# Weight sums made in DRAM by accumulating DMA, for a Strassen form that only adds, and a projection half that begins with the kept weights

## The chip, the cores and the metric

The kernel runs on one core of one Trainium2 chip. The metric is device microseconds of one execution; a profile is one further execution, taken by the hardware profiler. The engines that matter here: TensorE (PE) multiplies, with its weight loads counted apart (PEld); VectorE (DVE), ScalarE (ACT) and GpSimd (POOL) work elementwise; SyncE (SP) computes nothing and issues most transfers. POOL issues some transfers on a queue of its own. Sixteen DMA engines carry all of them.

## The reference

One layer of a hybrid encoder is computed for two groups that share weights: a prompt of 1024 rows and a sample of 64 rows, 1088 columns in all in the kernel's transposed layout, model width 1024, float32.

- Conditioning: `mod = silu(c) @ w_ada + b_ada` gives shift, scale and gate for both sub-layers (adaLN).
- Token mixing: `u = rmsnorm(x) * (1 + sc1) + sh1`, `proj = u @ w_in`; from `proj` come a stick-breaking attention (8 heads of 64) and an mLSTM (4 heads of 128, in chunks). Both are projected (`w_a`, `w_b`), gated by sigmoids, merged, and `x = x + g1 * (merged @ w_out)`.
- Channel mixing: `u2 = rmsnorm(x) * (1 + sc2) + sh2`; `x = x + g2 * ((silu(u2 @ w_ff_gate) * (u2 @ w_ff_up)) @ w_ff_down)`, inner width 2816, which is 22 blocks of 128.
- A last rmsnorm. Keys, values, states and convolution rows are outputs too.

## The kernel before

Every product is made from pairs of fp32r tiles: a high part (a rounded copy, the helpers `hi_act`, L46, and `hi_pool`, L52) and a low part (the rest, `lo_dve`, L55, and `lo_pool`, L58), with three matmuls high-high, high-low, low-high (`mm3`, L74). A weight block of 1024 x 128 is loaded as a raw tile (tag `wr`, three buffers of 512 KB), then split into tags `wh` and `wl` (three buffers each).

**The order of the work** is not the program's order line by line. A planner walks the written program with costs of its own: each engine takes, whenever it is free in the plan, the instruction that comes first in the program among those whose inputs and buffers are ready. The result is a fixed order per engine; on the chip each engine keeps it and waits where it must.

**Start** (to about 72 us). The rows of x are loaded, normalised and transposed. The adaLN weights of the first two of six parts are loaded in blocks (`ada_blocks`, L180, tiles `wada`, ten buffers, L187), two blocks for each of the eight row blocks of the input (`ada_pair`). `make_u` (L271) modulates block kb and splits it into `uh` (POOL, L52) and `ul` (DVE, L55). The q and k units of mLSTM head 0 accumulate over kb as the blocks come. The gates' weights are loaded at L855.

**mLSTM stage** (to about 480 us). Four heads; for each, a consumer (`mlstm(h)`) is woven by `run` (L814) into a list of dense units: the attention's q, k, v of pair h (`qkv_units`, L792) and the mLSTM units of head h + 1 (`ml_units`, L797). A unit is one weight block against all columns in three chunks (`unit`, L313, load at L63). Then come the attention stage and the two branch projections.

**Output projection** (about 957 to 1079 us). The eight output blocks m are made twice: first for columns 0 to 543 (`wo_weights`, `residual`, `wo_half(m, 0, ...)`), then for the rest (`wo_half(m, 1, ...)`, loop at L1185), each half in two quarters of 272 columns (`wo_quarter`, L1043), with the residual add on DVE (L1051) and squares summed on POOL (L1059). In the second loop each weight block is loaded and split again (L1187). While it runs, `todo` modulates the first half for the FFN (`rstd_rows`, `modulate2`, L1130), one step after each quarter, and writes the seven operand pairs of a Strassen product (`split`, `ops`).

**Gate and up** (about 1079 to 1584 us). For each of the 22 FFN blocks i, the gate weights (A11, A12: the two row halves) and the up weights (A21, A22) form one 2 x 2 block matrix against the input's 2 x 2 blocks, and Strassen's form with seven products (Winograd's variant) is used: `order = (1, 6, 5, 7, 2, 3, 4)`. `load_pair` (L1207) loads the two raw tiles; `weight_op` (L1217) makes the sums S1, S2, S3 of weight quarters on POOL (L1228, L1229, L1235, L1240) and splits each of the seven weights with ACT and DVE; `gate_up` (L1253) issues 84 matmuls for one half of the columns (L1289) and recombines the products on DVE, ACT and POOL (L1264 to L1282), storing h to DRAM (L1283). The order of the 44 half jobs: blocks 0 to 9 first half, blocks 10 to 21 both halves, blocks 0 to 9 second half; so the weights of blocks 0 to 9 are made twice. The weights of the next job are made, one by one, after each product of the present job (`hook`). The modulation of the second column half is stepped in the first ten jobs at products 1, 5 and 2.

**Down projection and output** (to the end) are untouched by the change.

Of the kernel before, what the change touches and what calls it, by code (L numbers as in the profile page):

```python
# [8 lines left out]
F32 = mybir.dt.float32  # L9
# [5 lines left out]
P = 128  # L15
# [4 lines left out]
KB = 8  # L20
# [2 lines left out]
TILES = [(0, 64)] + [(64 + 128 * i, 128) for i in range(8)]  # L23
CTILES = [(0, 1, 2), (3, 4, 5), (6, 7, 8)]
FFB = 22
HT = T // 2
QT = T // 4
XW = 3 + NS + 3 + NP
# [6 lines left out]
def trunk(ctx, tc, a, o, dbg=None, stop=None):  # L35
# [9 lines left out]
    def hi_act(out, in_):  # L45
        nc.scalar.copy(out, in_)  # L46
# [23 lines left out]
    def cols(w, c0, n=P):  # L70

        return w[:, c0 : c0 + n].rearrange("(kb p) n -> p kb n", p=P)
# [72 lines left out]
    gb_d = dram.tile([KB, P, T], F32, name="gb_d")  # L145
    pb_d = dram.tile([KB, P, T], F32, name="pb_d")
    nm_d = dram.tile([36, P], F32, name="nm_d")

    def small(shape, name, tag, dtype=F32, bufs=2, pool=None):
        return (pool or cur["sb"]).tile(shape, dtype, tag=tag, name=name, bufs=bufs)  # L150
# [892 lines left out]
    def wo_quarter(m, q, ws):  # L1043
# [9 lines left out]
        if m == 0:  # L1053
# [4 lines left out]
        if m < KB - 1:  # L1058
            nc.gpsimd.tensor_add(acc[:, s:e], acc[:, s:e], sq)  # L1059
        return sq  # L1060

    def wo_half(m, h, ws, after):
        sq = []
        for i in range(2):
            sq.append(wo_quarter(m, 2 * h + i, ws))
            if i == 1:
                nc.sync.dma_start(x1_d[m][:, HT * h : HT * (h + 1)], x1v(m, HT * h, HT * (h + 1)))
            after()
        return sq

    def rstd(accs, c, name):
# [48 lines left out]

    ops = {}

    def split(h, jp, p, src):
# [4 lines left out]
    def modulate2(h, jp, r):  # L1130


        x = [x1t[h, jp, i] for i in range(2)]
        rr = r.rearrange("p i t -> p (i t)")
        for i in range(2):
            nc.vector.tensor_mul(x[i], x[i], rr[:, None, :].to_broadcast([P, 2, HT]))
# [11 lines left out]
        nc.vector.tensor_sub(t2, b22, b11)  # L1148
        split(h, jp, 5, b11)
        yield  # L1150
        nc.vector.tensor_sub(b11, b21, t2)
# [20 lines left out]
        next(gen, None)  # L1172

    order = (1, 6, 5, 7, 2, 3, 4)
    sqs = None
    for m in range(KB):
        ws, xr = wo_weights(m)
        for c in range(3):
            residual(m, c, xr)
        sqs = wo_half(m, 0, ws, lambda: None)  # L1180
# [4 lines left out]
    for m in range(KB):  # L1185
        raw = wp.tile([P, KB, P], F32, tag="wr", name=f"wr_wp{m}")
        nc.sync.dma_start(raw, cols(w_out, m * P))  # L1187
        ws = [wp.tile([P, KB, P], F32R, tag=t, name=f"{t}_wp{m}") for t in ("wh", "wl")]
        hi_act(ws[0], raw)
        lo_pool(ws[1], raw, ws[0])  # L1190
        sqs = wo_half(m, 1, ws, lambda: step(todo))
    for _ in todo:
        pass
    for p in order:
# [10 lines left out]
        return gp.tile([P, QT], F32, tag=tag, name=name, bufs=1)  # L1205

    def load_pair(i):  # L1207
        raws = []
        for w, nm in ((w_g, "g"), (w_u, "u")):
            raw = wp.tile([P, KB, P], F32, tag="wr", name=f"wr_{nm}{i}")  # L1210
            nc.sync.dma_start(raw, cols(w, i * P))
            raws.append(raw)
        return [raws[0][:, 0:4], raws[0][:, 4:8], raws[1][:, 0:4], raws[1][:, 4:8]]

    S = {}

    def weight_op(i, p, raw):  # L1217

        a11, a12, a21, a22 = raw

        def new(tag):
            return gp.tile([P, 4, P], F32, tag=tag, name=f"{tag}_{i}", bufs=1)

        if p == 1:
            src = a11
        elif p == 6:
            S[1], S[2] = new("S1"), new("S2")
            nc.gpsimd.tensor_add(S[1], a21, a22)  # L1228
            nc.gpsimd.tensor_sub(S[2], S[1], a11)  # L1229
            src = S[2]  # L1230
        elif p == 5:
            src = S[1]
        elif p == 7:
            src = new("S3")
            nc.gpsimd.tensor_sub(src, a11, a21)  # L1235
        elif p == 2:
            src = a12
        elif p == 3:
            src = new("S3")
            nc.gpsimd.tensor_sub(src, a12, S[2])  # L1240
        else:
            src = a22
        k = order.index(p)
        if k < 6:
            w = wp.tile([P, KB, P], F32R, tag="wh" if k < 3 else "wl", name=f"w{p}_{i}")
        else:
            w = npl.tile([P, T], F32R, tag="acc", name=f"w{p}_{i}", bufs=1)[:, : KB * P].rearrange("p (k n) -> p k n", n=P)
        w = w.rearrange("p (x j) n -> p x j n", x=2)
        hi_act(w[:, 0], src)
        lo_dve(w[:, 1], src, w[:, 0])  # L1250
        return w

    def gate_up(i, h, ws, after):  # L1253
# [7 lines left out]
        def evac(p):  # L1261
            if p == 1:
                t["p1"] = tq("p1", f"p1_{i}_{h}")
                nc.scalar.copy(t["p1"], ba)  # L1264
            elif p == 6:
                t["u2"] = tq("u2", f"u2_{i}_{h}")
                nc.vector.tensor_add(t["u2"], bb, t["p1"])
            elif p == 5:
                nc.vector.tensor_add(h1, bc, t["u2"])  # L1269
            elif p == 7:  # L1270
                nc.vector.tensor_add(h1, bd, h1)
            elif p == 2:
                t["g0"] = tq("g0", f"g0_{i}_{h}")
                nc.scalar.activation(t["g0"], ba, AF.Silu)
            elif p == 3:
                t["g1"] = tq("g1", f"g1_{i}_{h}")
                nc.vector.tensor_add(t["g1"], bc, t["u2"])
                nc.scalar.activation(t["g1"], t["g1"], AF.Silu)  # L1278
                nc.gpsimd.tensor_mul(h1, t["g1"], h1)  # L1279
            else:  # L1280
                nc.vector.tensor_add(h0, bd, t["u2"])  # L1281
                nc.vector.tensor_mul(h0, t["g0"], h0)  # L1282
                nc.sync.dma_start(h_d[i][:, HT * h : HT * (h + 1)], hst)  # L1283

        for p in order:
# [19 lines left out]
            yield  # L1305


    NF = 10
# [205 lines left out]
```

## Time and profile before

| | |
|---|---|
| three runs, median | 1879.35 us (1872.82 to 1879.62) |
| profiled execution | 1873.3 us, span 1871.6 us |
| mean granted TensorE clock | 0.978 |
| PE busy | 1774.8 us, 95% |
| DVE, ACT, POOL busy | 1010.6, 667.9, 812.6 us |
| read from DRAM, written to it | 171.46 MB, 56.83 MB |

A busy PE is not a PE at its peak: its matmuls overlap, and at a lowered clock each lasts longer. The number of matmuls in a stretch, set against the stretch's length, tells more. DMA share and GB/s of a stretch tell how full the DMA engines are. Waits are put down to the semaphore that came last.

### The profile page before, as it was taken

Reading aid. Unit: us, or ns where it says so; the run is one execution under the profiler, and the core shown is the slowest. Engines: PE = TensorE matmul, PEld = TensorE weight load, DVE = VectorE, ACT = ScalarE, POOL = GpSimd, SP = SyncE. Lnnn points to the kernel's source line nnn. Section 1 sums busy time; section 2 is a strip of 40 time slices with the busy share of each in tenths; the row PEclk is TensorE's granted clock in tenths of the full one; section 3 lists DMA queues with packets and bytes.
Section 4 is the critical chain, followed back from the end, with each engine's and each line's share of the span. In section 5 each row is a group of like instructions: output and inputs, shape, how many; then the busy total and the mean of one; then the engine's idle time right before and its main releaser. Section 6 shows DMA issues by size and latency. Waiting matters only on the chain. (4 is left out here: it accounts for less than half of the span.)

```text
span 1871.6 us, 31615 instructions
## 1 busy us (share of the span) xinstructions
PE 1774.8 (95%) x12388; PEld 1700.0 (91%) x12388; DVE 1010.6 (54%) x1859; ACT 667.9 (36%) x1404; POOL 812.6 (43%) x665
## 2 busy tenths in 40 slices
PE   6999999999899999979989988999999998999997
PEld 4799999999898888868989988999999988999997
DVE  6623324242367586876461888654444765444535
ACT  4423434342244444534223554432333443100006
POOL 3433435352423222496665645542233456354323
PEclk9999999999999999989999979999999999999999
DMA  9323433324855565764665323332223433543102
GB/s 274 100 87 92 111 92 103 101 84 138 180 139 133 146 145 143 200 203 137 197 193 158 93 75 103 115 98 70 76 70 93 139 110 112 191 144 115 58 12 96
DMA packets 277575, 230.36 MB, mean 123 GB/s; under 512 B 11830, under 2 KB 255794, under 8 KB 277426
## 3 DMA queue, kind: packets, MB, share of 16 engines
q1 hardware_dynamic: 271794, 210.51, 38.2%
q0 software_dynamic: 5632, 17.83, 4.3%
q8 instruction: 98, 1.61, 0.4%
q14 instruction: 51, 0.42, 0.1%
HBM read 171.46 MB, written 56.83 MB: 122 GB/s over the span
## 5 line engine op out<-in xcount | busy, mean ns | idle before, releaser
L77 PE MATMUL ps_fd<-hh,wl_fd 128*128 128x384 f32 (+1 forms) x480 | 157.3, 328 | 2.1 <-POOL wl_fd L58 2.1
L75 PE MATMUL ps_fd<-hh,wh_fd 128*128 128x384 f32 (+1 forms) x480 | 157.1, 327 | 0.6 <-DVE hst L1281 0.6
L76 PE MATMUL ps_fd<-hl,wh_fd 128*128 128x384 f32 (+1 forms) x480 | 157.0, 327 | 0.0
L55 DVE TENSOR_TENSOR w<-S,w 128x512 fp32r<-128x512 f32 x128 | 104.8, 833 | 61.5 <-ACT w L46 59.9
L46 ACT CAST w<-S 128x512 fp32r<-128x512 f32 x128 | 76.8, 619 | 134.4 <-POOL S L1229 44.3
L1366 DVE SCALAR_TENSOR_TENSOR x1f<-ps_fd,mod,x1f 128x384 f32<-128x384 f32 (+2 forms) x128 | 60.5, 497 | 101.7 <-PE ps_fd L77 101.6
L363 DVE TENSOR_TENSOR_SCAN re<-re 128x128 f32<-128x128 f32 (+3 forms) x64 | 106.7, 1670 | 15.9 <-ACT re L359 15.5
L1240 POOL TENSOR_TENSOR S<-wr_g,S 128x512 f32<-128x512 f32 x32 | 49.1, 1536 | 126.4 <-DVE w L55 126.4
L77 PEld LDWEIGHTS ps_fd<-hh,wl_fd 128*128 128x128 f32 x480 | 90.1, 188 | 2.4 <-POOL wl_fd L58 2.4
L75 PEld LDWEIGHTS ps_fd<-hh,wh_fd 128*128 128x128 f32 x480 | 90.1, 188 | 0.8 <-issue 0.8
L76 PEld LDWEIGHTS ps_fd<-hl,wh_fd 128*128 128x128 f32 x480 | 90.1, 188 | 0.0
L46 ACT CAST hh<-hr 128x1088 fp32r<-128x1088 f32 (+1 forms) x26 | 24.0, 961 | 177.5 <-PE ps_fd L76 148.0
L1289 PE MATMUL ps_gb<-b6h,w 128*128 128x272 f32 x352 | 78.4, 301 | 6.0 <-DVE w L55 3.2
L1289 PE MATMUL ps_gc<-b3h,w 128*128 128x272 f32 x352 | 76.3, 296 | 8.2 <-DVE hst L1269 7.7
L1289 PE MATMUL ps_ga<-b1h,w 128*128 128x272 f32 x352 | 75.1, 292 | 5.0 <-DVE x L1051 5.0
L1228 POOL TENSOR_TENSOR S<-wr_u 128x512 f32<-128x512 f32 x32 | 42.4, 1325 | 83.8 <-DMA wr_u<-in_w_ff_up 74.8
L359 ACT ACTIVATE re<-z 128x512 f32<-128x512 f32 (+2 forms) x96 | 47.3, 494 | 82.2 <-DVE z L355 66.5
L1289 PE MATMUL ps_gc<-b5h,w 128*128 128x272 f32 x352 | 76.2, 295 | 0.0
L1289 PE MATMUL ps_gd<-b7h,w 128*128 128x272 f32 x352 | 74.8, 291 | 0.8 <-ACT w L46 0.8
L1289 PE MATMUL ps_ga<-b2h,w 128*128 128x272 f32 x352 | 74.7, 290 | 0.0
L1289 PE MATMUL ps_gd<-b4h,w 128*128 128x272 f32 x352 | 73.7, 289 | 0.0
L1279 POOL TENSOR_TENSOR hst<-g,hst 128x272 f32<-128x272 f32 x44 | 37.1, 843 | 81.7 <-ACT g L1278 81.7
(544 smaller groups left out, 6223.1 us busy)
## 6 DMA issues: line engine op xcount, KB each, us to landing
wada<-in_w_ada SPq DMA_DIRECT2D x48, 512.0 KB
wr_g<-in_w_ff_gate SPq DMA_DIRECT2D x32, 512.0 KB
wr_u<-in_w_ff_up SPq DMA_DIRECT2D x32, 512.0 KB
h_d<-hst SPq DMA_DIRECT2D x44, 272.0 KB
wr_fd<-in_w_ff_down SPq DMA_DIRECT2D x20, 512.0 KB
hr<-h_d SPq DMA_DIRECT2D x18, 544.0 KB
qs<-qk_d POOLq DMA_DIRECT2D x16, 272.0 KB, 6.9
kh<-qk_d POOLq DMA_DIRECT2D x16, 272.0 KB, 4.3
```

What stands on the lines that cost most here:

```text
L46: nc.scalar.copy(out, in_)
L55: nc.vector.tensor_sub(out, in_, h.bitcast(F32))
L75: nc.tensor.matmul(ps, wh, xh, start=first, stop=False)
L76: nc.tensor.matmul(ps, wh, xl, start=False, stop=False)
L77: nc.tensor.matmul(ps, wl, xh, start=False, stop=last)
L359: nc.scalar.activation(rest[:, c0 : c0 + w], ps, AF.Sigmoid, scale=-scale)
L363: nc.vector.tensor_tensor_scan(r, r, r, 1.0, ALU.mult, ALU.bypass)
L1228: nc.gpsimd.tensor_add(S[1], a21, a22)
L1240: nc.gpsimd.tensor_sub(src, a12, S[2])
L1279: nc.gpsimd.tensor_mul(h1, t["g1"], h1)
L1289: nc.tensor.matmul(ps, w[:, a, j, :], b[j // 2][:, j % 2, :], start=p in (1, 6, 5, 7) and j == 0 and k == 0, stop=j == 3 and k == 2, skip_ ...
L1366: nc.vector.scalar_tensor_tensor(x1[m][:, lo:hi], ps[:, lo - s : hi - s], mod[:, 40 + m, g : g + 1], x1[m][:, lo:hi], ALU.mult, ALU.add)
```

## The change

Three parts.

1. For blocks 0 to 9 (the first 1280 columns of the gate and up weights) four sums of weight quarters are made once, in DRAM: `wsum1 = u1 + u2`, `wsum2 = g1 + wsum1`, `wsum3 = u1 + g1`, `wsum4 = g2 + wsum2`, where 1 and 2 are the upper and lower 512 rows. Each is a copy from DRAM to DRAM issued on SP (`sum_copy`, two transfers of 512 x 640) and an accumulating transfer issued on POOL (`sum_add`, two transfers). In the program they stand between the dense units of the mLSTM heads: all copies with head 0, the adds 1 and 3 with head 1, add 2 with head 2, add 4 with head 3. `load_pair` for these blocks loads seven quarters of 256 KB, three of them straight from the weights and four from the sums, into three `wr` tiles and the tile S1; `weight_op` then only splits.
2. The signs are changed so that the weight sums are sums alone: the block operands b and the recombination on DVE take the sign. The product that ends h for the second row half moves from POOL to DVE, and both closing products become scalar_tensor_tensor with -1. Blocks 10 to 21 still make their sums on POOL, as additions. The second half's modulation is stepped at products 6 and 2 of the first ten jobs.
3. The second loop of the output projection runs over m in the order 7, 6, 5, 0, 1, 2, 3, 4; for 7, 6 and 5 it uses the weight tiles that the first loop still holds. Three steps of `todo` are taken for each m in place of two.

```diff
+    wsum_d = {x: dram.tile([KH, NFC], F32, name=f"wsum{x}_d") for x in (1, 2, 3, 4)}
+    g1w, g2w, u1w, u2w = w_g[0:KH, 0:NFC], w_g[KH:D, 0:NFC], w_u[0:KH, 0:NFC], w_u[KH:D, 0:NFC]
+    sum_parts = {1: (u1w, u2w), 2: (g1w, wsum_d[1]), 3: (u1w, g1w), 4: (g2w, wsum_d[2])}
+    def sum_copy(x):
+        def go():
+            for c in range(0, NFC, NFC // 2):
+                nc.sync.dma_start(wsum_d[x][:, c : c + NFC // 2], sum_parts[x][0][:, c : c + NFC // 2])
...
+    def sum_add(x):
+        def go():
+            for c in range(0, NFC, NFC // 2):
+                nc.gpsimd.dma_start(wsum_d[x][:, c : c + NFC // 2], sum_parts[x][1][:, c : c + NFC // 2], accum_op=ALU.add)
...
     for h in range(4):
-        dense = qkv_units(h) + (ml_units(h + 1) if h < 3 else ada_left[0:2] + gates[0:2])
+        q_, k_, kp, v_, vp = qkv_units(h)
+        m_ = ml_units(h + 1) if h < 3 else ada_left[0:2] + gates[0:2]
+        b_ = [[sum_copy(1), sum_copy(3), sum_copy(2), sum_copy(4)], [sum_add(1), sum_add(3)], [sum_add(2)], [sum_add(4)]][h]
+        dense = []
+        for i, g in enumerate([q_, k_, kp, v_, vp] + m_):
+            dense += [g] + (b_[i // 2 : i // 2 + 1] if i % 2 == 0 else [])
         run(mlstm(h), chain(dense), 14, 23 if h < 3 else 17)
...
-        nc.vector.tensor_sub(b11, b12, b11)
+        nc.vector.tensor_sub(b11, b11, b12)
...
+    def some(i):
+        step(todo)
+        if i == 1:
+            step(todo)
+
+    again = (7, 6, 5, 0, 1, 2, 3, 4)
+    for m in again:
+        ws = kept[m]
+        if m < 5:
+            raw = wp.tile([P, KB, P], F32, tag="wr", name=f"wr_wp{m}")
+            nc.sync.dma_start(raw, cols(w_out, m * P))
...
+        sqs = wo_half(m, 1, ws, m == again[0], m == again[-1], some)
...
+        src = {1: half(w_g, 0), 6: half(wsum_d[2], 0), 5: half(wsum_d[1], 0), 7: half(wsum_d[3], 0),
+               2: half(w_g, 1), 3: half(wsum_d[4], 0), 4: half(w_u, 1)}
+        for k in range(4):
+            if k < 3:
+                raw = wp.tile([P, KB, P], F32, tag="wr", name=f"wr_{k}_{i}")
+            else:
+                raw = gp.tile([P, 4, P], F32, tag="S1", name=f"wr_{k}_{i}", bufs=1)
+            for x, p in enumerate(order[2 * k : 2 * k + 2]):
+                res[p] = raw[:, 4 * x : 4 * x + 4]
+                nc.sync.dma_start(res[p], src[p])
...
-        if p == 1:
-            src = a11
+        if i < NF or p in (1, 2, 4):
+            src = raw[p]
...
-                nc.gpsimd.tensor_mul(h1, t["g1"], h1)
+                nc.vector.scalar_tensor_tensor(h1, h1, -1.0, t["g1"], ALU.mult, ALU.mult)
             else:
                 nc.vector.tensor_add(h0, bd, t["u2"])
-                nc.vector.tensor_mul(h0, t["g0"], h0)
+                nc.vector.scalar_tensor_tensor(h0, h0, -1.0, t["g0"], ALU.mult, ALU.mult)
...
-            if (k < NF and p in (1, 5, 2)) or (k >= FFB and p == 5):
+            if (k < NF and p in (6, 2)) or (k >= FFB and p == 5):
                 step(todo)
```

More of the change, by code (lines that the diff above doesn't have):

```diff
@@ L1041, in residual, with wo_quarter @@
             nc.scalar.copy(x1v(m, lo, hi), pst[:, lo - s : hi - s])
-    def wo_quarter(m, q, ws):
+    def wo_quarter(m, q, ws, first, last):
         (wh, wl), s, e = ws, QT * q, QT * (q + 1)
@@ L1052, in wo_quarter @@
         x = x1v(m, s, e)
-        if m == 0:
+        if first:
             nc.scalar.activation(acc[:, s:e], x, AF.Square)
@@ L1057, in wo_quarter, with wo_half @@
         nc.scalar.activation(sq, x, AF.Square)
-        if m < KB - 1:
+        if not last:
             nc.gpsimd.tensor_add(acc[:, s:e], acc[:, s:e], sq)
         return sq
-    def wo_half(m, h, ws, after):
+    def wo_half(m, h, ws, first, last, after):
         sq = []
         for i in range(2):
-            sq.append(wo_quarter(m, 2 * h + i, ws))
+            sq.append(wo_quarter(m, 2 * h + i, ws, first, last))
             if i == 1:
                 nc.sync.dma_start(x1_d[m][:, HT * h : HT * (h + 1)], x1v(m, HT * h, HT * (h + 1)))
-            after()
+            after(i)
         return sq
@@ L1184, in trunk @@
     todo = chain([rstd_rows(0, sqs, rows2[0], sbank), modulate2(0, 0, rows2[0]), modulate2(0, 1, rows2[0])])
[L1185 to L1191, printed above, removed]
+    def some(i):
[8 more added lines that the diff above has]
+            nc.sync.dma_start(raw, cols(w_out, m * P))
+            ws = [wp.tile([P, KB, P], F32R, tag=t, name=f"{t}_wp{m}") for t in ("wh", "wl")]
+            hi_act(ws[0], raw)
+            lo_pool(ws[1], raw, ws[0])
+        sqs = wo_half(m, 1, ws, m == again[0], m == again[-1], some)
     for _ in todo:
@@ L1207, in load_pair, with half @@
     def load_pair(i):
[L1208 to L1213, printed above, removed]
+        def half(w, r):
+            return w[r * KH : (r + 1) * KH, i * P : (i + 1) * P].rearrange("(k p) n -> p k n", p=P)
+        res = {}
+        if i >= NF:
+            raws = []
+            for w, nm in ((w_g, "g"), (w_u, "u")):
+                raw = wp.tile([P, KB, P], F32, tag="wr", name=f"wr_{nm}{i}")
+                nc.sync.dma_start(raw, cols(w, i * P))
+                raws.append(raw)
+            res[1], res[2], res[0], res[4] = raws[0][:, 0:4], raws[0][:, 4:8], raws[1][:, 0:4], raws[1][:, 4:8]
+            return res
+        src = {1: half(w_g, 0), 6: half(wsum_d[2], 0), 5: half(wsum_d[1], 0), 7: half(wsum_d[3], 0),
[8 more added lines that the diff above has]
+                nc.sync.dma_start(res[p], src[p])
+        return res
     S = {}
     def weight_op(i, p, raw):
[L1219 removed]
         def new(tag):
             return gp.tile([P, 4, P], F32, tag=tag, name=f"{tag}_{i}", bufs=1)
[L1224 to L1225 removed]
+        if i < NF or p in (1, 2, 4):
+            src = raw[p]
         elif p == 6:
             S[1], S[2] = new("S1"), new("S2")
[L1228 to L1229 removed]
+            nc.gpsimd.tensor_add(S[1], raw[0], raw[4])
+            nc.gpsimd.tensor_add(S[2], S[1], raw[1])
             src = S[2]
@@ L1234, in weight_op @@
             src = new("S3")
[L1235 to L1238, printed above, removed]
+            nc.gpsimd.tensor_add(src, raw[1], raw[0])
+        else:
             src = new("S3")
-            nc.gpsimd.tensor_sub(src, a12, S[2])
-        else:
-            src = a22
+            nc.gpsimd.tensor_add(src, raw[2], S[2])
         k = order.index(p)
```

22 lines of the change are left out of this document (15 added, 7 removed).

## The prediction

> **What bounds the kernel now.** I read the page first, for the share of each engine, and then the windows, stage by stage, because a kernel whose TensorE (PE) is 95% busy can only change where PE is not fed.
>
> ```profile
> span 1871.6 us, 31615 instructions
> PE 1774.8 (95%) x12388; PEld 1700.0 (91%) x12388; DVE 1010.6 (54%) x1859; ACT 667.9 (36%) x1404; POOL 812.6 (43%) x665
> ```
>
> In the windows a row begins with the stretch and its length; then come busy time and instruction count for PE, its weight loads, DVE, ACT and POOL; then the granted clock, the DMA share and GB/s. These rows go from the end of the second projection half through the whole gate/up stage:
>
> ```profile
> 1033.00:1074.00 41.00, 41.00 (x329) 40.85 (x328) 38.27 (x38) 25.23 (x48) 25.90 (x17) 1.00 0.33 100
> 1074.00:1079.50 5.50, 0.48 (x5) 0.29 (x3) 4.85 (x7) 1.88 (x5) 5.04 (x5) 0.77 0.14 51
> 1079.50:1101.00 21.50, 21.50 (x135) 21.14 (x136) 13.63 (x24) 11.87 (x22) 5.47 (x5) 0.74 0.21 62
> 1101.00:1143.00 42.00, 33.36 (x233) 32.04 (x232) 41.97 (x56) 24.55 (x46) 19.93 (x14) 0.90 0.26 77
> 1143.00:1206.00 63.00, 61.98 (x467) 61.18 (x466) 45.87 (x76) 26.30 (x54) 34.59 (x27) 0.96 0.40 119
> 1206.00:1227.00 21.00, 20.11 (x152) 19.12 (x152) 11.12 (x22) 6.95 (x16) 11.48 (x10) 1.00 0.45 128
> 1227.00:1480.00 253.00, 253.00 (x2015) 253.00 (x2014) 128.54 (x239) 85.01 (x169) 81.42 (x72) 1.00 0.28 86
> 1480.00:1584.00 104.00, 98.93 (x741) 94.05 (x740) 66.43 (x115) 41.03 (x85) 54.55 (x44) 1.00 0.40 116
> ```
>
> The undisturbed row is 1227 to 1480: 2015 matmuls in 253 us, 125.6 ns each, so a half job of 84 takes 10.55 us. I price every other row by its count, since "busy" hides slow matmuls. The loss is 5.5 - 5 x 0.1256 = 4.9 us, then 4.5, 12.7, 4.3, 1.9, and 10.9 in the last row: 39.2 us. The projection (1033 to 1074) loses nothing. Two causes show. From 1101 to 1143 DVE is busy 41.97 of 42 us: it is the bound. And its instructions are stretched there, as the groups of the same two windows show (mean ns after the comma), first the crowded stretch, then the calm one:
>
> ```profile
> L55 DVE TENSOR_TENSOR w<-S,w 128x512 fp32r<-128x512 f32 x10 | 9.6, 971 | 0.0
> ...
> L55 DVE TENSOR_TENSOR w<-S,w 128x512 fp32r<-128x512 f32 x51 | 36.7, 720 | 9.3 <-ACT w L46 8.7
> ```
>
> In the last ten half jobs the bound is a chain instead: the load of the up weights lands late, and three POOL sums of 1.29 us follow before ACT and DVE can split them.
>
> ```profile
> L1240 POOL TENSOR_TENSOR S<-wr_g,S 128x512 f32<-128x512 f32 x8 | 14.0, 1747 | 13.7 <-DVE w L55 13.7
> L1229 POOL TENSOR_TENSOR S<-S,wr_g 128x512 f32<-128x512 f32 x8 | 10.3, 1292 | 0.0
> L1235 POOL TENSOR_TENSOR S<-wr_g,wr_u 128x512 f32<-128x512 f32 x8 | 10.3, 1289 | 0.0
> L1228 POOL TENSOR_TENSOR S<-wr_u 128x512 f32<-128x512 f32 x8 | 10.3, 1288 | 22.8 <-DMA wr_u<-in_w_ff_up 16.9 <-DVE hst L1271 5.9
> ```
>
> The start is a third kind of stretch. The first row is mostly the rows of x, the second the adaLN weights, the third what comes behind them:
>
> ```profile
> 4.00:14.00 10.00, 2.50 (x14) 2.39 (x15) 3.41 (x11) 8.23 (x17) 0.00 (x0) 1.00 1.01 393
> 35.00:57.00 22.00, 21.19 (x219) 16.99 (x208) 10.43 (x18) 5.80 (x7) 9.29 (x8) 0.90 1.07 264
> 57.00:70.00 13.00, 12.85 (x106) 11.64 (x99) 7.90 (x21) 4.73 (x6) 3.30 (x3) 1.00 0.16 40
> ```
>
> Up to 57 us the DMA engines are full (the last columns are their share and GB/s); then they are nearly idle.
>
> **What the change gains in gate/up.** In the twenty half jobs of blocks 0 to 9 the four POOL sums go, so DVE runs unstretched and the last ten lose their chain. The price is traffic. A job loads seven quarters of 256 KB (1.84 MB) in place of 1.05 MB, and stores 0.28 MB: 2.11 MB in 10.55 us is 200 GB/s, and the start of this kernel moves 264. I cost this at nothing; the cover is one job of lead, and below 200 GB/s each job would lengthen. The product moved from POOL to DVE costs about what its neighbour L1282 costs, and both lie on a DVE that must be counted:
>
> ```profile
> L1269 DVE TENSOR_TENSOR hst<-ps_gc,u 128x272 f32<-128x272 f32 x24 | 10.6, 441 | 12.1 <-PE ps_gc L1289 10.9
> L1282 DVE TENSOR_TENSOR hst<-g,hst 128x272 f32<-128x272 f32 x23 | 10.2, 446 | 1.4
> L1136 DVE TENSOR_TENSOR x<-x,rr 128x1088 f32<-128x1088 f32 x4 | 4.9, 1288 | 1.6 <-ACT rr L1118 1.6
> L1148 DVE TENSOR_TENSOR t<-x,x 128x544 f32<-128x544 f32 x2 | 1.4, 716 | 0.0
> ```
>
> Seven splits of 0.72, five evacuations of 0.44 and two products of 0.45 are 8.1 us a job. The modulation of the second half (4.9 us, then 22 instructions of 0.71) is 20.5 us; spread over ten jobs instead of seven it adds 2.1: 10.2 of 10.55 us. That is nearly full, so I leave 4 us of loss, and 3 us for the row-sum matmuls and a clock that drops after them. Gain: 39.2 - 7 = **32 us**. The bounds are 16 (DVE stays the bound in the first ten jobs) and 39.
>
> **The projection half** drops three loads, three ACT casts and three POOL subtractions, all hidden today (329 x 0.1256 = 41.3 us in 41). Its modulation steps come earlier, which serves the DVE backlog behind the 4.9 us after 1074; that term is in the sum already. Nothing more is taken.
>
> **Where the sums are made.** This term decides. Eight copies of 512 x 640 floats (1.31 MB; 10.49 MB in all) are written into SP's program between the units of the first mLSTM head, and eight adds on POOL later. But the order on an engine is not the program's:
>
> ```profile
> L565 DVE TENSOR_TENSOR icol<-g_if,bif x2: 193/798/1404, 90.2 to 91.9; 64x4 f32<-64x4 f32 x1, 128x32 f32<-128x32 f32 x1
> L558 DVE MEMSET icol<- x1: 62/62/62, 1.6 to 1.6; 64x4 f32 x1
> ```
>
> The memset at L558 stands seven lines above L565 in the gates' code, yet ran at 1.6 us and not near 90: it needs nothing, so the planner placed it as soon as the engine was free. SP does likewise at the start:
>
> ```profile
> 16.22 0.58 SPq L63 DMA_DIRECT2D wr_mq<-in_w_in  x1
> ...
> 34.18 1.60 SPq L855 DMA_DIRECT2D wif_raw<-in_w_in  x1
> ...
> 38.79 0.39 SPq L63 DMA_DIRECT2D wr_mv<-in_w_in  x1
> 39.28 2.14 SPq L187 DMA_DIRECT2D wada<-in_w_ada  x2
> 41.52 1.72 SPq L63 DMA_DIRECT2D wr_mo<-in_w_in  x1
> 43.33 5.19 SPq L187 DMA_DIRECT2D wada<-in_w_ada  x3
> 48.62 1.95 SPq L63 DMA_DIRECT2D wr_q<-in_w_in  x1
> 50.66 1.69 SPq L187 DMA_DIRECT2D wada<-in_w_ada  x1
> 52.45 1.69 SPq L63 DMA_DIRECT2D wr_k<-in_w_in  x1
> ```
>
> The adaLN loads (wada, ten buffers) come before wif_raw in the program; once ten were out, wif_raw, wr_mv, wr_mo, wr_q went ahead of the last six. So in the plan SP had gaps there, filled with whatever was ready. wr_k, which the new program places behind the first copy, was issued right after the last wada. The copies need no buffer and no earlier result. I therefore expect all eight between wr_mv and the last wada. And there the DMA engines are full, as the row 35 to 57 above shows.
>
> No copy from DRAM to DRAM is in this trace. At the 393 GB/s of the x rows it takes 26.7 us, at the 264 of the stretch where it will lie 39.7, and twice 26.7 = 53.4 if reading and writing DRAM count separately. I take 40, by the nearest row.
>
> The wait it makes: modulated block kb of the input needs its wada pair, and every later matmul needs all eight blocks, so PE has nothing else.
>
> ```profile
> 22.95 1.06 POOL L52 TENSOR_SCALAR wh_mq<-wr_mq 128x1024 fp32r<-128x1024 f32 x1 [21.08 <-DMA wr_mq<-in_w_in]
> 61.21 0.84 PE L190 MATMUL ps_ada<-wada,cT 128*32 128x128 f32 x18
> q1 hardware_dynamic: 271794, 210.51, 38.2%
> q0 software_dynamic: 5632, 17.83, 4.3%
> L403 POOL DMA_DIRECT2D kh<-qk_d x16: 509/542/588, 483.8 to 777.4; - x16
> DMA to landing us min/median/max: 3.6/6.9/17.1
> ```
>
> From issue to use wr_mq took 6.7 us (16.22 to 22.95), so the last wada, issued at 50.66, lands near 57.4 and is used at 61.2: 4 us to spare.
>
> The adds go through POOL's queue q0. Today it moved 17.83 MB in 4.3% of 1871.6 us, 221 GB/s. Adds 1 and 3 (5.24 MB) can go once their copies land, also ahead of the last wada: 23.7 us at that rate, 47.4 if an add must read its target too, nothing if they come later. I take 12, half of the first. Issuing costs POOL 0.54 us each; behind a waiting add stand the casts uh of the input blocks, and DVE and PE wait for those. Adds 2 and 4 fall where POOL and DMA are idle enough (DMA share 0.16 from 57 us).
>
> The Trainium skill ("DMA: Bandwidth & Descriptors", Specifications) gives about 358 GB/s of HBM per core; by that, as an estimate, the copies, read and written, take 58.6 us and the total would be 1911. Its section "Queues, rings and completion order" says that an engine alternates between queues packet by packet; by that, 2560-byte rows of an add hold back 512-byte rows of a wada for the add's whole length, 12 us more than I take. The landings above, 3.6 to 17.1 us for equal transfers, bear this out in kind.
>
> Loss at the start: 40 + 12 - 4, and 3 for a lowered clock after the idle time (0.74 in the row after 1074's stall): **51 us**.
>
> **The sum.** Profiled 1873.3 us (span 1871.6) - 32 + 51 = **1892 us**. The runs' median is 1879.35 (1872.82 to 1879.62), so the profile is a quick one; the same shift on the median gives 1898.
>
> **Rivals.**
> - *Cheap copies.* At 27 us, with the adds after the last wada, the loss is 27 - 4 + 3 = 26 and the result 1867, or up to 1883 with a part of the adds. For it: the 393 GB/s row. Against: those are loads into SBUF. This is no change within what a measurement can tell (0.5%, 9.4 us). 0.18.
> - *Copies behind the last wada* (faster). If the plan leaves SP no free slot before that load, they fall after 57 us, where the DMA share is 0.16 and 10.49 MB delay nobody. Only the gain is left: 1873.3 - 32 = 1841. The point that decides is the copies' place in SP's order relative to the row at 50.66. For it: nothing shows SP idle in the plan directly. Against: the memset and wif_raw. 0.22.
> - *POOL held up too.* Copies at 53, both early adds at 47 and in front of the casts: 53 + 47 - 4 + 3 - 32 = +67, 1940. 0.12.
> - *The sums do not free the first ten jobs.* 10.2 of 10.55 us is too tight, only 16 us is gained: 1873.3 - 16 + 51 = 1908. 0.10.
>
> **How the numbers follow.** My forecast, 1884 to 1905, has 0.38. Slower: 0.38 + 0.12 + 0.10 = 0.60; same 0.18; faster 0.22. The range 1836 to 1930 takes in the faster rival and most of the slower ones; the forecast's own range is 1884 to 1905.
>
> **What would show it.** Right: SP's copies between wr_mv and the last wada; that wada issued at 85 to 105 us, not 50.66; DMA share near 1 from 57 to 90; PE idle there; later, rows of 84 matmuls per 10.55 us in the last ten jobs and little POOL. Wrong: the last wada still near 50 (then 1841), or DVE at full share in the first ten jobs with matmuls still missing.

## The result and the profile after

The changed kernel takes 1888.55 us (median of five, 1886.90 to 1891.88) against 1874.48 us for the kernel before beside it (1872.82 to 1879.62): a ratio of 1.0068, 95% interval 1.0047 to 1.0089. It is slower, by 0.7%. The profiled execution took 1888.55 us, with a span of 1886.8.

The page's first rows, and its queues and traffic:

```profile
span 1886.8 us, 31673 instructions
PE 1766.3 (94%) x12388; PEld 1701.0 (90%) x12388; DVE 1000.8 (53%) x1903; ACT 670.5 (36%) x1401; POOL 664.6 (35%) x546
...
q1 hardware_dynamic: 305218, 235.16, 42.0%
q0 software_dynamic: 9856, 28.32, 7.3%
...
HBM read 206.59 MB, written 77.81 MB: 151 GB/s over the span
```

PE does the same 12388 matmuls in less busy time, POOL is relieved by 148 us, and yet the span is 15.2 us longer. So the reader has to go by stages. Where a stage begins is read from the first matmul of a tile (operations and count, then min/median/max ns, then the start of the first and of the last one). The three tiles are ps_if, the gates of the mLSTM, which need all eight input blocks; ps_wo, the output projection; and ps_fd, the down projection. Before, and then after:

```profile
L548 PE MATMUL ps_if<-uh,wif x24: 304/334/522, 72.0 to 83.9; 128*16 128x384 f32 x16, 128*16 128x320 f32 x8
L75 PE MATMUL ps_wo<-mh,wh_wo x128: 283/288/575, 957.9 to 1020.2; 128*128 128x272 f32 x128
L75 PE MATMUL ps_fd<-hh,wh_fd x480: 305/334/384, 1584.0 to 1824.5; 128*128 128x320 f32 x80, 128*128 128x384 f32 x80
```

```profile
L573 PE MATMUL ps_if<-uh,wif x24: 304/332/338, 125.5 to 133.0; 128*16 128x384 f32 x16, 128*16 128x320 f32 x8
L76 PE MATMUL ps_wo<-mh,wh_wo x176: 283/288/428, 1008.4 to 1094.8; 128*128 128x272 f32 x176
L76 PE MATMUL ps_fd<-hh,wh_fd x480: 302/334/383, 1601.7 to 1839.8; 128*128 128x320 f32 x80, 128*128 128x384 f32 x80
```

The same three starts cut every profile of this study into four stretches. This table is worked out from them (a stretch is the difference of two starts; the last runs to the end of the span):

| kernel | ps_if starts | to ps_wo | to ps_fd | to the end | span |
|---|---|---|---|---|---|
| before | 72.0 | 885.9 | 626.1 | 287.6 | 1871.6 |
| after | 125.5 | 882.9 | 593.3 | 285.1 | 1886.8 |
| e1: copies held | 70.7 | 925.3 | 592.1 | 285.1 | 1873.2 |
| e2: sums made, not used | 124.5 | 885.7 | 624.8 | 289.1 | 1924.1 |
| e3: copies alone | 98.2 | 886.3 | 625.7 | 289.1 | 1899.3 |
| e4: other edits alone | 72.4 | 887.5 | 626.6 | 289.9 | 1876.4 |
| e5: copies and adds held | 70.7 | 872.6 | 593.9 | 285.2 | 1822.4 |
| e6: adds held | 98.4 | 877.4 | 596.0 | 285.1 | 1856.9 |
| e7: as e5, steps as before | 71.2 | 876.4 | 592.0 | 285.1 | 1824.7 |
| e8: as e2, small adds | 102.7 | 880.7 | 625.6 | 289.2 | 1898.2 |
| e9: as e2, both held | 70.8 | 880.3 | 624.8 | 289.2 | 1865.1 |
| e10: held copies, small adds | 72.1 | 889.1 | 627.0 | 289.3 | 1877.5 |

After against before: 53.5 us lost before ps_if, 32.8 gained from the output projection to the end of gate/up, 3.0 and 2.5 in the other two stretches; 53.5 - 38.3 = 15.2.

**Where the time went.** The windows of the start and SP's issues in it, of after:

```profile
35.00:57.00 22.00, 19.08 (x202) 15.59 (x195) 12.26 (x22) 7.96 (x11) 13.70 (x11) 0.97 0.95 281
57.00:70.00 13.00, 4.67 (x40) 3.90 (x38) 0.88 (x1) 0.00 (x0) 1.54 (x2) 0.88 1.10 215
70.00:100.00 30.00, 7.41 (x36) 6.17 (x36) 2.28 (x5) 1.57 (x2) 2.13 (x2) 0.56 1.06 282
```

```profile
40.19 0.39 SPq L64 DMA_DIRECT2D wr_mv<-in_w_in  x1
40.63 1.25 SPq L161 DMA_DIRECT2D wsum_d<-in_w_ff_up  x2
41.97 0.60 SPq L212 DMA_DIRECT2D wada<-in_w_ada  x1
42.62 5.43 SPq L161 DMA_DIRECT2D wsum_d<-in_w_ff_up  x1
48.15 1.12 SPq L212 DMA_DIRECT2D wada<-in_w_ada  x1
49.31 5.87 SPq L161 DMA_DIRECT2D wsum_d<-in_w_ff_up  x1
55.23 27.18 SPq L161 DMA_DIRECT2D wsum_d<-in_w_ff_gate  x4
82.51 6.54 SPq L64 DMA_DIRECT2D wr_mo<-in_w_in  x1
89.15 17.69 SPq L212 DMA_DIRECT2D wada<-in_w_ada  x3
106.93 1.63 SPq L64 DMA_DIRECT2D wr_q<-in_w_in  x1
108.65 1.58 SPq L212 DMA_DIRECT2D wada<-in_w_ada  x1
```

All eight copies stand between wr_mv and the last wada, as forecast. From 57 to 100 us PE has 76 matmuls in 43 us and the DMA engines are full. SP itself stands 27.18 us in the issue of four copies, so the loads behind them are not even issued; the last wada is issued at 108.65 us, before at 50.66. What PE waits for there, in order of time:

```profile
74.37 0.44 PE L215 MATMUL ps_ada<-wada,cT 128*32 128x128 f32 x4 [12.70 <-DMA wada<-in_w_ada]
85.44 0.64 PE L76 MATMUL ps_mx<-uh,wh_mq 128*128 128x320 f32 x1 [8.76 <-POOL uh L53]
108.83 0.44 PE L215 MATMUL ps_ada<-wada,cT 128*32 128x128 f32 x4 [17.75 <-DMA wada<-in_w_ada]
```

The middle wait is for a cast on POOL that stands behind an add (e8 comes back to it); the first and the last are for adaLN weights.

**Where it came from.** The first matmul of gate/up, before and then after; and then, of after, the first ten half jobs and the last ten:

```profile
1079.46 0.56 PE L1289 MATMUL ps_ga<-b1h,w 128*128 128x272 f32 x1 [5.02 <-DVE x L1051]
```

```profile
1126.03 0.36 PE L1341 MATMUL ps_ga<-b1h,w 128*128 128x272 f32 x1 [0.72 <-DVE x L1081]
```

```profile
1126.00:1243.00 117.00, 115.05 (x889) 114.29 (x890) 93.22 (x176) 68.07 (x131) 5.92 (x5) 0.97 0.62 180
1485.00:1590.00 105.00, 105.00 (x839) 105.00 (x838) 77.67 (x147) 55.42 (x106) 0.00 (x0) 1.00 0.69 206
```

PE's wait in front of the first job, 5.02 us before, is now 0.72. The first ten jobs lose 117 - 889 x 0.1256 = 5.3 us, and the last ten nothing: 839 x 0.1256 = 105.4 us in 105, with POOL empty and the DMA engines moving 206 GB/s. Of the 5.3 us PE stands idle 2.0 (117 - 115.05), and its waits there name ACT (1.8 and 0.2 us); the rest are matmuls that last longer, at a granted clock of 0.95 from 1126 to 1190 us.

### The profile page after: what moved, and what is told of

It is laid out like the page before. It is cut to its first block, busy times and chain, and to the rows that moved or that the text cites. A ratio compares the mean times of both kernels' runs of the same rounds, so it can differ in the third digit from the quotient of the medians.

```text
span 1886.8 us, 31673 instructions
## 1 busy us (share of the span) xinstructions
PE 1766.3 (94%) x12388; PEld 1701.0 (90%) x12388; DVE 1000.8 (53%) x1903; ACT 670.5 (36%) x1401; POOL 664.6 (35%) x546
## 3 DMA queue, kind: packets, MB, share of 16 engines
HBM read 206.59 MB, written 77.81 MB: 151 GB/s over the span
## 5 line engine op out<-in xcount | busy, mean ns | idle before, releaser
L56 DVE TENSOR_TENSOR w<-wr,w 128x512 fp32r<-128x512 f32 x140 | 95.4, 691 | 39.4 <-ACT w L47 36.4
L388 DVE TENSOR_TENSOR_SCAN re<-re 128x128 f32<-128x128 f32 (+3 forms) x64 | 107.3, 1679 | 13.3 <-ACT re L384 12.9
L47 ACT CAST w<-wr 128x512 fp32r<-128x512 f32 x140 | 85.1, 619 | 69.6 <-PE ps_gd L1341 17.7
L53 POOL TENSOR_SCALAR wh_fd<-wr_fd 128x1024 fp32r<-128x1024 f32 x20 | 24.6, 1232 | 227.6 <-PE ps_ga L1341 119.4
L215 PE MATMUL ps_ada<-wada,cT 128*32 128x128 f32 x768 | 43.1, 309 | 33.8 <-DMA wada<-in_w_ada 33.5
L1341 PE MATMUL ps_gb<-b6h,w 128*128 128x272 f32 x352 | 74.4, 290 | 0.2 <-ACT g L1326 0.2
L215 PEld LDWEIGHTS ps_ada<-wada,cT 128*32 128x32 f32 x768 | 23.2, 119 | 49.5 <-issue 26.5
```

Source lines behind the costliest of these rows:

```text
L53: nc.gpsimd.tensor_scalar(out, in_, 1.0, 0.0, ALU.mult, ALU.add)
L56: nc.vector.tensor_sub(out, in_, h.bitcast(F32))
L215: nc.tensor.matmul(ps[g : g + 32, b * P : (b + 1) * P], cT[:, kb, :], raw[:, kb, :], start=kb < 4, stop=kb >= 4, tile_position=(0, g))
L388: nc.vector.tensor_tensor_scan(r, r, r, 1.0, ALU.mult, ALU.bypass)
L1341: nc.tensor.matmul(ps, w[:, a, j, :], b[j // 2][:, j % 2, :], start=p in (1, 6, 5, 7) and j == 0 and k == 0, stop=j == 3 and k == 2, skip_ ...
```

## The experiments

My theory was the prediction's: the sums gain some 33 us in gate/up, and the place of the copies and adds in the full start costs more. The rivals: the other edits make the gain; or the transfers cost their time wherever they lie; or POOL, standing at an add, makes the wait.

**e1: the copies hold their written place.** Every instruction whose place is not fixed is set by the planner; here the copies' places in SP's order are fixed, so that they come behind the last wada.

```diff
-                nc.sync.dma_start(wsum_d[x][:, c : c + NFC // 2], sum_parts[x][0][:, c : c + NFC // 2])
+                tc.keep_in_program_order(nc.sync.dma_start(wsum_d[x][:, c : c + NFC // 2], sum_parts[x][0][:, c : c + NFC // 2]))
```

> The changed kernel, but each of the eight copies holds its written place in SP's order, which is behind the last wada load and between the units of the first head. Theory (the place of the copies at the DMA-full start costs the time, the sums themselves gain): the last wada is issued near 50.7 us as before, the first ps_if matmul is at 72 +- 2 us, and with the 38 us that the changed kernel gained after it the time is 1836 to 1845 us. Rival A (the 10.49 MB of copies and 10.49 MB of adds cost about the same wherever they lie): the loss of 53 us comes again, in the first head, and the time is near 1888. Rival B (a part of it is a cost of the adds on POOL): 1850 to 1870.

Measured: 1879.56 us against 1878.68, ratio 0.9998 (0.9985 to 1.0012). All three expectations miss in part. The start is as before (ps_if at 70.7) and gate/up is as short as in the changed kernel, but the stretch from ps_if to ps_wo is 39.4 us longer. The loss has moved, not gone. The groups of waits of PE from 130 to 240 us name one ACT copy for both large gaps (us in total, times, longest):

```profile
PE ps_q L76 <- ACT co L770: 20.4, 1, 20.4
PE ps_nat_k L363 <- ACT co L770: 9.8, 1, 9.8
```

That is only the last link. What ACT and DVE themselves stood at shows more (rows of the timeline, with the idle time before and what ended it), beside the windows of these places:

```profile
151.37 0.48 ACT L47 CAST sh<-ps_k 128x384 fp32r<-128x384 f32 x1 [13.75 <-DMA qk_d<-sh]
237.43 0.17 DVE L725 TENSOR_TENSOR dc<-W,mcb 128x8 f32<-128x8 f32 x1 [26.09 <-DMA W<-nm_d]
```

```profile
130.00:160.00 30.00, 20.22 (x113) 18.86 (x112) 2.42 (x8) 5.63 (x15) 5.83 (x5) 0.83 1.05 265
...
200.00:225.00 25.00, 19.41 (x120) 19.05 (x118) 4.22 (x12) 1.68 (x4) 9.92 (x8) 0.99 1.10 236
225.00:240.00 15.00, 0.18 (x1) 0.21 (x2) 1.94 (x4) 2.24 (x5) 5.39 (x8) 0.50 0.85 180
```

The adds had followed their copies into the first head, at 136 to 222 us. There a store of 192 KB (qk_d) and a load of 576 KB (W) stand in a tight chain, and both landed late: W was issued at 209.97 and used at 237.43, 27.5 us later; in the kernel before it took 7.4 (192.16 to 199.51).

**e2: the sums are made and not used.** The kernel before, with the change's `sum_copy` and `sum_add` at the same places.

```diff
-        dense = qkv_units(h) + (ml_units(h + 1) if h < 3 else ada_left[0:2] + gates[0:2])
+        b_ = [[sum_copy(1), sum_copy(3), sum_copy(2), sum_copy(4)], [sum_add(1), sum_add(3)], [sum_add(2)], [sum_add(4)]][h]
+        dense = []
+        for i, g in enumerate([q_, k_, kp, v_, vp] + m_):
+            dense += [g] + (b_[i // 2 : i // 2 + 1] if i % 2 == 0 else [])
```

> The kernel before, with the eight copies and eight adds emitted as in the change; gate/up forms its own sums as before and nothing reads the sums in DRAM. Theory: only the start changes, ps_if at 125 +- 3 us, time 1874 + 53 = 1927 (1920 to 1933). Rival (the change's other edits move the start, or the traffic in gate/up hides a gain): less than 1915 or more than 1940.

Measured: 1925.36 us, ratio 1.0261 (1.0235 to 1.0286), ps_if at 124.5. Of the 53.5 us lost in the start, 52.5 come with making the sums alone; the other edits have at most 1 us in it.

**e3: copies alone.** As e2, without the adds.

```diff
-        b_ = [[sum_copy(1), sum_copy(3), sum_copy(2), sum_copy(4)], [sum_add(1), sum_add(3)], [sum_add(2)], [sum_add(4)]][h]
+        b_ = [[sum_copy(1), sum_copy(3), sum_copy(2), sum_copy(4)], [], [], []][h]
```

> The kernel before with the eight copies and no adds; what is copied is not read. It tells the copies' part of the loss from the adds' part. By the prediction's terms (copies 40, slack 4, clock 3) the time is 1874 + 39 = 1913, the last wada is issued near 90 us. If add 3, on which POOL waited 22 us with a cast of the input behind it, is the larger part: 1890 to 1900. If the adds cost nothing: 1925 to 1930.

Measured: 1900.98 us, ratio 1.0125 (1.0110 to 1.0140); ps_if at 98.2. Here the prediction's term fell: the copies cost 26.2 us, not 39, and the adds in the changed kernel another 27.3, not 12. The time lies just above the range for the adds as the larger part; the two parts are about equal. A window and SP's rows of e3 show how the start differs without adds:

```profile
57.00:70.00 13.00, 6.86 (x43) 5.64 (x41) 2.28 (x5) 1.57 (x2) 1.10 (x1) 0.87 1.04 347
```

```profile
53.00 8.48 SPq L159 DMA_DIRECT2D wsum_d<-in_w_ff_gate  x4
...
80.83 1.62 SPq L210 DMA_DIRECT2D wada<-in_w_ada  x1
```

The engines move 347 GB/s, where with adds among the copies (row 57 to 70 of after) they move 215 at the same full share; and SP is through with the four copies in 8.48 us instead of 27.18.

**e4: the other edits alone.** The changed kernel without copies, adds and sums in DRAM; all 22 blocks make their sums on POOL.

```diff
-        b_ = [[sum_copy(1), sum_copy(3), sum_copy(2), sum_copy(4)], [sum_add(1), sum_add(3)], [sum_add(2)], [sum_add(4)]][h]
+        b_ = []
...
-        if i >= NF:
+        if True:
...
-        if i < NF or p in (1, 2, 4):
+        if p in (1, 2, 4):
```

> The changed kernel without copies, adds and sums in DRAM: all 22 blocks form their sums on POOL as before, while the sign of the operands, the product on DVE, the steps after two products in place of three and the kept projection weights stay. Theory (the gain in gate/up comes from the sums): start as before (ps_if at 72), 3 us gained in the projection, the last ten half jobs 11.7 to 12.1 us as before, time 1860 to 1874. Rival (the gain comes from steps, product and kept weights): 1836 to 1845, as with the sums.

Measured: 1880.84 us against 1878.68, ratio 1.0012 (1.0000 to 1.0023). The stretch to ps_fd is 626.6 us, before 626.1. The time is above the theory's range too: the theory holds on where the gain comes from, the sums, but its 3 us in the projection do not show. Signs, product on DVE, steps and kept weights are worth nothing without the sums. That includes the gap at 1074, which I had put down to the modulation: with the earlier steps and the kept weights, but without the sums, PE still stands 5.21 us there, as e4's first matmul of gate/up shows.

```profile
1081.39 0.57 PE L1341 MATMUL ps_ga<-b1h,w 128*128 128x272 f32 x1 [5.21 <-DVE x L1081]
```

**e5: copies and adds both hold their written places.** As e1, and the adds too, which puts adds 1 and 3 into the second head, add 2 into the third and add 4 into the fourth.

```diff
-                nc.gpsimd.dma_start(wsum_d[x][:, c : c + NFC // 2], sum_parts[x][1][:, c : c + NFC // 2], accum_op=ALU.add)
+                tc.keep_in_program_order(nc.gpsimd.dma_start(wsum_d[x][:, c : c + NFC // 2], sum_parts[x][1][:, c : c + NFC // 2], accum_op=ALU.add))
```

> The changed kernel, with copies and adds both held in their written places: copies behind the last wada, adds 1 and 3 behind the first head's casts of weights on POOL, adds 2 and 4 in the third and fourth head. With the copies alone held (e1) the start was as before and gate/up 34 us shorter, but 39 us went in the first head: 10.0 and 20.6 us of PE idle time just as POOL stood at an add that waited for its copy, with wh_mk and wh_k behind it. Theory (that loss is POOL's wait in front of the weight casts): an add held behind finds its copy landed, nothing waits, and the time is 1878.7 - 34 + 0 to 8 = 1845 to 1853. Rival (10.49 MB of copies on SP's queue delay the loads and stores of the first head whatever POOL does): 1865 to 1885.

Measured: 1830.30 us against 1878.42, ratio 0.9751 (0.9729 to 0.9774). This is faster than both kernels, and 15 us below the range that I expected. Where the copies run (100 to 200 us) and the first adds (203 to 227), PE now stands nowhere, and the DMA share is 0.55 to 0.70:

```profile
100.00:130.00 30.00, 30.00 (x185) 29.10 (x184) 7.46 (x25) 9.52 (x25) 11.54 (x14) 1.00 0.55 181
130.00:200.00 70.00, 70.00 (x454) 68.89 (x453) 23.58 (x51) 19.97 (x49) 23.47 (x21) 1.00 0.67 208
200.00:280.00 80.00, 80.00 (x513) 78.60 (x512) 26.22 (x52) 31.75 (x70) 38.62 (x35) 1.00 0.70 170
```

The time doesn't tell whether POOL's wait or the transfers made e1's loss; e10 does. The 13.3 us beyond the sum are in the stretch from ps_if to ps_wo, where no sum is used; e9 is about them.

**e6: the adds alone hold their places,** and the copies stay in the start (the edit of e5 without that of e1).

> The changed kernel with the adds alone held in their written places; the copies stay among the wada loads at the start. The copies alone delayed ps_if by 26 us (e3), copies and adds by 53. Theory (the other 27 us are the adds, through bandwidth and through POOL's 22 us wait with a cast of the input behind it): ps_if near 98, time 1878.7 + 26 - 34 = 1871 (1867 to 1876). Rival (the adds cost their transfer time wherever they run): 1885 to 1895, as the changed kernel.

Measured: 1857.39 us, ratio 0.9892 (0.9871 to 0.9912). ps_if is at 98.4, as expected and as in e3: the adds' 27 us are not paid a second time where they now lie. The total is 14 us below my figure and 10 below its range: 8.5 of it is again in the stretch from ps_if to ps_wo.

**e7: as e5, with the modulation's steps as before.**

```diff
-            if (k < NF and p in (6, 2)) or (k >= FFB and p == 5):
+            if (k < NF and p in (1, 5, 2)) or (k >= FFB and p == 5):
```

> As e5 (copies and adds held in place), with the modulation of the second half stepped after products 1, 5 and 2 of a job, as before the change, and not after 6 and 2. The prediction put DVE at 10.2 of 10.55 us a job with two steps in ten jobs. With three the modulation (20.5 us) lies in seven jobs: 8.1 + 2.9 = 11.0 of 10.55 us, so 0.5 us too much in each of seven: theory 3 to 4 us slower than e5. Rival (DVE has slack, or the backlog is worked off behind PE): within 1 us of e5.

Measured: 1827.15 us (e5 1830.30), ratio to before 0.9730 (0.9712 to 0.9748). It is not slower, and the stretch with gate/up takes 592.0 us instead of 593.9. The theory of a nearly full DVE falls. DVE's share is in the row 1126 to 1243 of after: 93.22 of 117 us, 8.4 us per 10.55, where the prediction had 10.2.

**e8: as e2, with small adds.** Each add covers 64 of its 640 columns.

```diff
-                nc.gpsimd.dma_start(wsum_d[x][:, c : c + NFC // 2], sum_parts[x][1][:, c : c + NFC // 2], accum_op=ALU.add)
+                nc.gpsimd.dma_start(wsum_d[x][:, c : c + 64], sum_parts[x][1][:, c : c + 64], accum_op=ALU.add)
```

> As e2 (kernel before, copies and adds at the planner's places, nothing reads the sums), but each add covers 64 of its 640 columns: what the adds move falls from 10.49 to 1.05 MB, while POOL still stands at the same places in its order and waits for the same copies, with the uh casts behind. It tells apart why the adds cost 27 us beside the copies' 26 (e3 1901, e2 1925). Theory (transfer: the adds share the full DMA engines with copies and wada loads): near e3, 1899 to 1906. Rival (POOL's 22 us wait in front of a cast of the input): near e2, 1918 to 1926.

Measured: 1905.47 us, ratio 1.0147 (1.0126 to 1.0169), ps_if at 102.7. Of the 26.3 us by which the adds lengthen e2's start (98.2 to 124.5), 21.8 go with their bytes (124.5 to 102.7). The number of packets is the same (286022 in e2, 286023 in e8), so it is not their count. What POOL waited in front of the second transfer of add 3 went with the bytes; first the row of after, then that of e8:

```profile
83.25 1.00 POOL L169 DMA_DIRECT2D wsum_d<-in_w_ff_gate  x1 [22.22 <-DMA wsum_d<-in_w_ff_up]
```

```profile
63.07 1.00 POOL L167 DMA_DIRECT2D wsum_d<-in_w_ff_gate  x1 [5.51 <-DMA wsum_d<-in_w_ff_up]
```

So POOL's wait of 22 us was itself mostly an effect of the adds' transfers, which held back the copies that POOL waited for. How the delay reached PE, the trace of after tells (its three waits stand in the section on the result). After the 8.76 us at POOL's cast PE had work until 91 us only, and then stood 17.75 us at a wada load that SP had issued behind the copies. Between 50 and 109 us SP waited once for POOL, 2.9 us at a cast. So the delay came by way of the wada loads, but for these 2.9 us at most; the wait at the cast lay in its shadow. In e2 PE's waits are the same, 5.47 us at the cast and then 18.56 at wada.

**e9: both held, nothing used.** The kernel before with e5's copies and adds.

> The kernel before with copies and adds held in their written places as in e5; gate/up forms its own sums and nothing reads those in DRAM. e5 gained 33 us from the output projection on and 13 us more between the first ps_if matmul and the projection (872.6 us instead of 885.9), which nobody forecast. Theory (these 13 us come from another order of the work after the fourth head, which the held adds bring about, and not from the sums): 1860 to 1870, with 870 to 878 us between ps_if and ps_wo. Rival (they belong to the change's other edits): 1876 to 1882, with 884 to 888 us there.

Measured: 1868.06 us against 1877.03, ratio 0.9957 (0.9944 to 0.9971). The kernel gets faster by transfers that nobody reads. No arithmetic was taken from it, and the order of the work that the planner makes around the adds has changed in the fourth head. There POOL ran two products of the convolution (cv) before it cast the next weight block; in e9, as in e5, the second comes after the cast. First before, then e9:

```profile
413.47 2.55 POOL L673 TENSOR_TENSOR cv<-cv,cs 128x1091 f32<-128x1091 f32 x1 [1.52 <-ACT cs L672]
415.99 1.05 POOL L52 TENSOR_SCALAR wh_ga<-wr_ga 128x1024 fp32r<-128x1024 f32 x1
```

```profile
417.11 1.06 POOL L53 TENSOR_SCALAR wh_ga<-wr_ga 128x1024 fp32r<-128x1024 f32 x1 [2.01 <-DMA wr_ga<-in_w_in]
...
420.61 2.57 POOL L696 TENSOR_TENSOR cv<-cv,cs 128x1091 f32<-128x1091 f32 x1
```

The first matmul of the attention stage comes 434.1 us behind ps_if before (506.1 - 72.0), and 429.3 in both e9 and e5. That this order is the cause is the explanation left, not one that a run isolates. The stretch from ps_if to ps_wo is 880.3 us, not 870 to 878: 5.6 of e5's 13.3 us come without the sums being read; the other 7.7 stay open.

**e10: held copies, small adds at e1's places.** This tells the two accounts of e1 apart: POOL stands at the same adds, only the bytes are missing.

> The kernel before, copies held in their written places as in e1, adds at the planner's places in the first head (before the casts wh_mk and wh_k, as in e1) but of 64 of their 640 columns; nothing reads the sums. In e1 the stretch from the first ps_if matmul to the first of ps_wo took 925.3 us, 39 more than before (885.9). POOL stands at the same adds behind the same copies, only the adds' bytes are gone. Theory (transfer: copies and adds together fill the DMA engines, share 1.05 from 130 to 160 and 1.10 from 200 to 225, and the store qk_d and the load W of the head land late): 884 to 892 us there, time 1875 to 1885. Rival (POOL's wait with the weight casts behind it, as stated with e5): 915 to 927 us there, time 1905 to 1918.

Measured: 1876.75 us against 1876.62, ratio 1.0000 (0.9987 to 1.0014); 889.1 us from ps_if to ps_wo against e1's 925.3. POOL's rows of e1, then of e10, and e10's window:

```profile
136.08 1.24 POOL L169 DMA_DIRECT2D wsum_d<-in_w_ff_up  x1 [5.98 <-DMA wsum_d<-in_w_ff_up]
...
142.13 1.44 POOL L53 TENSOR_SCALAR wh_mk<-wr_mk 128x1024 fp32r<-128x1024 f32 x1
```

```profile
137.48 1.24 POOL L167 DMA_DIRECT2D wsum_d<-in_w_ff_up  x1 [5.89 <-DMA wsum_d<-in_w_ff_up]
...
142.09 1.44 POOL L53 TENSOR_SCALAR wh_mk<-wr_mk 128x1024 fp32r<-128x1024 f32 x1
```

```profile
130.00:160.00 30.00, 30.00 (x198) 28.92 (x197) 4.11 (x13) 9.71 (x29) 10.34 (x8) 1.00 1.00 288
```

POOL's wait at the first add is as long, it casts wh_mk at the same time, and PE is busy all 30 us. POOL's wait, the theory I had written for e5, did not make the loss of the first gap. The adds' bytes did, together with the copies'. The two instructions that stood at a DMA in e1 (13.75 and 26.09 us) stand much shorter in e10:

```profile
144.09 0.48 ACT L47 CAST sh<-ps_k 128x384 fp32r<-128x384 f32 x1 [5.07 <-DMA qk_d<-sh]
```

```profile
202.19 0.17 DVE L723 TENSOR_TENSOR dc<-W,mcb 128x8 f32<-128x8 f32 x1 [3.46 <-DMA W<-nm_d]
```

In front of the second gap POOL's waits at the adds shrank as well (19.5 us in e1, 8.7 in e10, four adds each), so there the two are less cleanly apart. But W is issued by SP, and its time from issue to use fell from 27.5 to 7.4 us (194.83 to 202.19), which is about the size of the gap of 20.4 us. Note that the DMA share is 1.00 in e10 from 130 to 160 us, while PE does not wait at all: a full share alone was no loss there.

## Why the prediction was right, and where it was right by luck

The forecast was 1892 with an own range of 1884 to 1905; the median is 1888.55. As a change it was 51 - 32 = 19 us; the spans give 15.2, the medians 14.1. The two terms came out at 53.5 - 32.8 = 20.7, and another 5.5 us were gained in the two stretches that the sum had at nothing. Point by point:

- **The place of the copies: right.** SP's order is the one forecast, and e2 shows that copies and adds at these places make the loss without the other edits. One sign was missed: the last wada was to be issued at 85 to 105 us and was issued at 108.65.
- **The size of the start's loss: 51 forecast, 53.5 measured, by two errors that cancel.** The step "copies 40" was too dear: with slack and clock it made 39, and e3 measured 26.2, near what the bound of 26.7 at 393 GB/s gives (26.7 - 4 + 3 = 25.7). I had chosen the 264 of the stretch where they would lie; with the copies in it, e3's engines moved 347 from 57 to 70 us. The slack of 4 and the 3 for the clock no run measures apart. The step "adds 12" was too cheap: e3 to after is 27.3. That is more than the whole of adds 1 and 3 at q0's rate (23.7), not half of it. All four transfers of adds 1 and 3 were issued ahead of the last wada (51 to 83 us), which was one of the two cases that I had split.
- **The rule on packets.** The Trainium skill ("DMA: Bandwidth & Descriptors", "Queues, rings and completion order") says that an engine alternates between queues packet by packet. I gave it 12 us more than I took for the adds, 24 together. The 27.3 us between e3 and after are near that, and in e8, where there are as many packets but those of the adds have a tenth of the length, 21.8 of e2's 26.3 us are gone; the alternation itself no run shows. The Trainium skill's 358 GB/s ("DMA: Bandwidth & Descriptors", Specifications), by which I estimated 58.6 us for the copies with reading and writing counted apart, is not borne out in that way of counting: copies alone cost 26.2.
- **The gain of 32: measured 32.8** (626.1 to 593.3), and e4 shows that it needs the sums. Inside it a step was wrong: the DVE at 10.2 of 10.55 us. It was 8.4, and e7's three steps a job cost nothing, so the 4 us set aside for it were not lost to DVE. What remains, 0.7 us in front of the first job and 5.3 in the first ten, is near the 7 left, but for other reasons in part: 2.0 us are waits for ACT, and some 3.4 us slow matmuls at the lowered clock, for which I had left 3.
- **Traffic at nothing: right.** 206 GB/s in the last ten jobs with no matmul missing.
- **The projection half at nothing: right** (e4). Only the reason given for the gap at 1074 was wrong: with the earlier steps alone it stays (5.21 us in e4), and with the sums read it closes (0.72). By which way the sums close it, no run shows.
- **The unforecast 2.5 us at the end.** All kernels that read the sums take 285.1 or 285.2 us from ps_fd on, all others 287.6 to 289.9; why, no run shows. The 3.0 us from ps_if to ps_wo are within what the order of the work moves there (872.6 to 889.1 in the kernels without e1's collision).
- **The rival "copies behind the last wada → 1841" had its condition met in e1, and its price was wrong.** I let 10.49 MB "delay nobody" because the share was 0.16 from 57 to 70 us. I hadn't followed the adds: they come as soon as the copies have landed, into the first head. With the adds held as well (e5) nothing is lost in the heads, and the time is 1830.30: 11 us below the price, by the 13.3 us that nobody forecast.

## What to carry to other kernels

A planner like this one puts work that needs no buffer and no earlier result as early as the queue allows, and a start that loads through full DMA engines is the worst place for it: here the same 21 MB cost 53 us there, 39 in the first head, and nothing when spread over four heads (e5, with a share of 0.55 to 0.70 in the first two). Before a transfer is called hidden, list its followers too, since an add issued by another engine moves with its copy. And when two terms of a sum are uncertain and could be exchanged, a total that comes out right proves neither; one run with one of them removed does.

## What the runs showed of the hardware

- Copies within DRAM delayed the start by 26.2 us for 10.49 MB (e3); in the window 57 to 70 us the engines moved 347 GB/s at a share of 1.04, each copied byte counted once (240.85 MB over the whole run, before 230.36). With adds among the copies (after) they moved 215 at 1.10.
- An issue can hold its engine long: SP stood 27.18 us in four copies and 17.69 in three wada loads; before, three wada loads took 5.19, and in e3 the four copies 8.48. In the changed kernel SP waited for no other engine in these two rows.
- The traffic counted as read grew by 35.1 MB (171.46 to 206.59) and as written by 21.0. The copies (10.49), the adds' sources (10.49) and the additional loads (20 x 0.786 - 3 x 0.524 = 14.2) make 35.2 already: reading the target of an accumulating transfer does not show in that count.
- A load of 576 KB beside copies and adds took 27.5 us from issue to use (W in e1, 209.97 to 237.43), beside copies and small adds 7.4 (e10), as before.
